# The third layer's recurrence by eights of chunks instead of chunk by chunk, with a new plan of the layer

## The chip, the cores and the metric

The kernel runs on one core of a Trainium2 chip. The metric is the device time of one execution in microseconds, as the median of several runs; a profiled execution gives the trace that is read here.

## The reference

One inference step of a network with four layers, on 128 context tokens and 512 latent tokens with 1,024 channels each (T = 640, E = 2,048). Every layer normalises its input, projects it, mixes the tokens in its own way, multiplies by SiLU(z), projects back and adds to the stream. The mixers are a Mamba-2 scan, a gated MLP over chunks, an S5 state-space layer, and neighbourhood attention. All is float32; each large product is done in three passes over split operands.

Only the third layer (S5) changes. For each of 128 groups of 16 channels there are 64 complex states, in two directions:

```python
bb = ...                         # the input matrix, discretised, per group and direction
drv = einsum('gnj,blgj->blgn', bb, seq)            # complex, in two real parts
drv[:, 0] += a * h0                                # the state from which the latent tokens start
s[l] = a * s[l - 1] + drv[l]                       # the recurrence over the tokens
y_d = einsum('gjn,blgn->blgj', c_re, s_re) - einsum('gjn,blgn->blgj', c_im, s_im)
y = gelu(y_forward + y_backward + d_skip * u)
y = y * sigmoid(y @ w_glu + b_glu) * silu(z)
```

The final states of the context are an output too.

## The kernel before

Tokens are taken in chunks of 8: 64 latent chunks and 16 of the context. TensorE takes each chunk's inputs to what they add to the states (`drive`), so that the recurrence runs over chunks only, with a to the power 8 (the tile `A8`). The 128 groups are worked in four quarters. A quarter's states lie in `S[(group of 2, state), direction, place, part, pair]`: on each partition 2 directions x 81 places x 2 parts x 16 pairs. `scan` is a generator of steps. A step of the latent chunks (`steps`, lines 1743 to 1753) is, for each direction, one product of the state (32 numbers) with both parts of A8 (64 results, tile `sl`, L1750) and two additions of 32 into the next place (L1753); all six are on VectorE, forward and backward in turn, and the next step needs them. There are 63 such steps in a quarter. Beside them GpSimd does the 16 steps of the context's chunks (`step`, tile `sc`: one product of 128, L1760, two additions of 64, L1762).

When a quarter's states are there, each of its four output matrices kt (8 groups) is made: `take` copies states into `zr` (ScalarE, one copy on GpSimd), `gen` makes the matrices from states to outputs by halves (`gx` and `gy`: seven operations of 512 elements on VectorE and five on GpSimd a kt, L1531 and L1544), `answer` multiplies on TensorE (L1805), `kernel` makes the response within a chunk (`KK`, eight DMAs to `tr`), and `within` multiplies (L1830), adds on VectorE (L1831) and applies GELU.

All this is laid beside the layer's large products (L314). A slot is one k tile of a product: six matmuls with 320 columns. `PLAN` gives the order of 28 of the first 32 products (16 of u, and z), 256 slots; the four last are z. The gate's products follow, 16 of them with 16 k tiles: the first 16 slots of these use y of matrices 0 to 7, the next those of 8 to 15. `put(slot, f)` puts a piece of work into the program after that slot. `SCAN5` has the first and last slot of each quarter's scan, `OUTS5` the slot o of a quarter's first output and the distance of the next ones, `OUT5` the slots of an output's parts after o, `IN5` those of a u product's loads (`ix`), transposes (`turn`) and drives after its end. TensorE, VectorE, ScalarE and GpSimd keep to the program's order in this layer; each runs until an operand is missing or a buffer isn't free. The numbers of buffers are `BG` (gx), `BM`, `BY` (gy) and `BI` (ix). The weights' parts (`whi` on ScalarE, `wlo` on GpSimd five times in six and on VectorE once) are made one product ahead. y goes to DRAM and comes back in another order (`load_y`, L1845, eight pairs of rows by 320-byte runs) for the gate.

Of the kernel before, what the change touches and what calls it, by code (L numbers as in the profile page):

```python
# [1 line left out]

# [29 lines left out]
# the steps of a layer's first product before the second's, by sides; a side's norm, by slots: the sums so far, the  # L32
# whole by tokens, by rows (the other side's from the next layer's beginning); its first operands; from where on the
# engines keep to the order
# [5 lines left out]
# token t of chunk c and place l in the third layer: column l * 80 + c, the latent chunks first  # L40
# [6 lines left out]
def reorder(perm, c, there, here):  # L47
    """A layer's columns of a part's tokens (0 the context's, 1 the latent ones), and these in the same order."""
    t0, t1 = ((0, TC), (TC, T))[c]
    if perm == 8:  # L50
        return there.rearrange("p (l c) -> p l c", l=8)[:, :, PERM[c]], here.rearrange("p (c l) -> p l c", l=8)
    there = there[:, t0:t1]
    if perm == -8 and c == 1:
        return there.rearrange("p (c r) -> p r c", r=8), here.rearrange("p (r c) -> p r c", r=8)
    return there, here
# [6 lines left out]
class Cut:  # L62
    """The tokens in two sides, between layers of these orders: the first side's last products come before the other's,
    and its next ones too. ys: a side's columns in the layer's order; hs: in the next's. A side's places are the natural
    order's: all has (first place, number, the columns of x, the places as these) for both parts; parts has them by part,
    with the next layer's columns; out: by part, with the products' columns in the layer's order."""

    def __init__(self, old, new):
# [19 lines left out]
        else:  # L88
            # the latent grid's columns from 32 on first
# [8 lines left out]
        if old == 8:  # L98
            # column l * 80 + r * 8 + q; in the natural order
# [18 lines left out]
class Net:  # L118
# [42 lines left out]
    def phase(self, name, side="left"):  # L161
        """A pool that lives as long as a part of a layer."""
# [5 lines left out]
    def x_tiles(self):  # L168
        """The residual stream, on the other side of the memory, from a layer's end into the next one."""
# [36 lines left out]
    def pcopy(self, o, a):  # L206
        """A copy on Pool."""
        self.nc.gpsimd.tensor_scalar(o, a, 1.0, 0.0, op0=OP.mult, op1=OP.add)

# [1 line left out]
    def raw(self, src, m=128):  # L211
        """src: a [128, 8, m] slice in DRAM."""
# [12 lines left out]
    def gemm(self, units, h, m=128):  # L225
        """units: weights' DRAM slices for the k tiles in eights; h(k) -> (hi, lo) [128, T]."""
# [15 lines left out]
    def stream(self, jobs, pairs=None, after=None, ahead=0, cut=None):  # L242
        """Products one after the other, the next weights' parts made ahead: jobs are (units, h, m, use), with
        use(the result). A generator, by k tiles. pairs: from there on, the first halves of two jobs come before their
        second ones. ahead: the weights' loads before their use. cut: the last product comes by sides, with use(the
        result, side)."""
# [76 lines left out]
    def play(self, jobs, at, pairs=None, also=(), after=None, cut=None, end=None):  # L323
        """The products, with other work (in program order) after some of their k tiles. also: other engines that
        keep to the program's order. after: the weights that are needed next."""
# [31 lines left out]
    def mod_w(self, i, nb, k, n, p, bufs, tag="wm"):  # L357
        """n k tiles' weights, from k on."""
# [4 lines left out]
    def mod_b(self, i, nb, q):  # L363
        """q [128, 4, 2]: a block's products."""
# [10 lines left out]
    def mod_pe(self, i, p, blocks=range(6), bufs=4, n=1):  # L375
        """On the tensor engine; a generator, by blocks."""
# [16 lines left out]
    def mod_ew(self, i, p, blocks=range(6), bufs=2, tags=("wm", "wacc"), pacc=None):  # L393
        """On the vector engine, but for turning the sums' partitions; a generator, in some more than four steps a
        block."""
# [43 lines left out]
    def put_beside(self, *work):  # L439
        """Work beside the present layer, by steps; the first layer's last modulation too, with its pool."""  # L440
# [4 lines left out]
    def tick(self, n):  # L445
        """Some steps of the work beside."""
        for g in self.beside:
            for _ in range(n):
                next(g, None)

# [1 line left out]
    def colsum(self, s):  # L452
        """s [128, T] -> the sums over its partitions, [token, chunk]."""
# [5 lines left out]
    def rowbc(self, r):  # L459
        """r [token, chunk] -> [128, T], the same on every partition."""  # L460
# [6 lines left out]
    def rstd(self, s, width):  # L467
        """s [128, T]: squares summed over the tiles -> 1/sqrt(mean + eps) on every partition."""
# [6 lines left out]
    def rstd_parts(self, s, width, out):  # L475
        """The same, into out; a generator, in two steps."""
# [7 lines left out]
    def rowcopy(self, r, out):  # L484
        """r [token, chunk] -> out [128, T], the same on every partition."""
# [11 lines left out]
    def square(self, k, t):  # L497
        """A tile's squares, to the sums over the tiles."""
# [18 lines left out]
    def enter(self, i, x, perm, ks):  # L517
        """The first layer's operands from its norm; the others' come with the layer before."""
# [19 lines left out]
    def side(self, i, x, s):  # L538
        """A side of the next layer's operands; a generator, by feature tiles."""
# [126 lines left out]
    def ordered(self, work):  # L666
        """In the program's order."""
# [5 lines left out]
    def norm_sums(self, s):  # L673
        """The squares' sums but for the last tile's."""
# [9 lines left out]
    def norm_tokens(self, s):  # L684
        """1/sqrt(mean + eps)"""
# [16 lines left out]
    def norm_rows(self, s):  # L702
        """The same on every partition."""
# [127 lines left out]
        # dt * decay to the end of the chunk (of the direction)  # L831
# [4 lines left out]
        # decay over a whole chunk, by step of the recurrence  # L836
# [6 lines left out]
        # decay by one token, to be broadcast: [dir, group, chunk, head, l]; none into a chunk's first token  # L843
# [1429 lines left out]
```

## Time and profile before

| | us |
|---|---|
| median of 3 runs | 3098.95 |
| lowest and highest | 3095.29, 3101.35 |
| profiled execution, first to last instruction (span) | 3088.6 |
| third layer, first u product to the gate's unbroken products | 1369 to 1953 |

The trace holds one execution; its time is given from the first instruction to the last. The runs' time is some 10 us longer, for what lies around these. Times in the rows below are microseconds from the span's start unless marked ns.

### The profile page before, as it was taken

What the parts mean: (1) busy time and instruction counts of PE and PEld (TensorE: products, weight loads), DVE (VectorE), ACT (ScalarE), POOL (GpSimd) and SP (SyncE); (2) the same over time, 40 slices, a digit from 0 to 9 for tenths busy, and PEclk for the clock granted to TensorE, in tenths of its full rate; (3) what the DMA queues carried; (4) which work ended last, traced back from release to release, by engine and by line L of the source; (5) the groups of instructions that cost most, each with busy time, mean ns of one, the idle gap of its engine ahead of it and who ended that gap; (6) DMA issues with size and microseconds to landing.
All of it is one profiled execution on the core that took longest, in us unless ns stands there. A gap on an engine that the chain in (4) does not pass through costs nothing.

```text
span 3088.6 us, 49942 instructions
## 1 busy us (share of the span) xinstructions
PE 2754.1 (89%) x18252; PEld 2663.7 (86%) x18252; DVE 2271.0 (74%) x5090; ACT 1319.5 (43%) x2359; POOL 1349.2 (44%) x1350
## 2 busy tenths in 40 slices
PE   7878887999989988989887867899999999999998
PEld 3868887889989988989887867899988999999988
DVE  7998777778789999983898893223965666667842
ACT  5422232331423333235545624445125666666641
POOL 4366656533276764443544543221434333333232
PEclk9989999999999999999988978899999999999999
DMA  6444334364433344545453536633634444444342
GB/s 249 121 128 118 115 107 116 99 219 161 150 112 126 124 143 154 194 148 184 133 178 116 161 109 149 148 108 102 201 121 128 134 133 135 135 135 135 109 174 86
DMA packets 248117, 432.17 MB, mean 140 GB/s; under 512 B 75264, under 2 KB 144320, under 8 KB 246848
## 3 DMA queue, kind: packets, MB, share of 16 engines
q1 hardware_dynamic: 247424, 427.66, 45.0%
q8 instruction: 145, 2.38, 0.3%
q0 software_dynamic: 448, 1.31, 0.1%
q14 instruction: 100, 0.82, 0.1%
HBM read 333.83 MB, written 65.70 MB: 129 GB/s over the span
## 4 chain that ended last, share of the span: by engine, by line
DVE 41%; PE 34%; issue 8%; ACT 8%; POOL 4%; DMA 4%; SPq 1%; DVEq 0%; ACTq 0%; POOLq 0%
PE acc L314 26%; DVE wacc L426 6%; DVE S L1753 4%; DVE cacc L902 3%; DVE sl L1750 3%; DVE wlo L204 2%; ACT whi L203 2%; DVE dd L1012 1%; DVE s5gx L1544 1%; DVE dd L1014 1%; DVE s5gx L1534 1%; POOL dd L1016 1%; ACT e L2054 1%; POOL dd L1009 1%; DVE Bu L1507 1%
## 5 line engine op out<-in xcount | busy, mean ns | idle before, releaser
L314 PE MATMUL acc<-hhi,whi 128*128 128x320 f32 (+2 forms) x3472 | 863.5, 328 | 27.9 <-DVE x L597 9.4
L314 PE MATMUL acc<-hhi,wlo 128*128 128x320 f32 (+2 forms) x3472 | 821.7, 316 | 10.8 <-DVE wlo L204 9.5
L314 PE MATMUL acc<-hlo,whi 128*128 128x320 f32 (+2 forms) x3472 | 824.0, 317 | 6.0 <-DVE hlo L566 3.7
L204 POOL TENSOR_TENSOR wlo<-raw,whi 128x1024 fp32r<-128x1024 f32 x157 | 400.2, 2551 | 694.9 <-ACT whi L203 681.0
L314 PEld LDWEIGHTS acc<-hhi,whi 128*128 128x128 f32 (+1 forms) x3472 | 602.4, 196 | 37.4 <-ACT hhi L203 16.6
L314 PEld LDWEIGHTS acc<-hhi,wlo 128*128 128x128 f32 (+1 forms) x3472 | 600.4, 193 | 14.5 <-DVE wlo L204 11.1
L314 PEld LDWEIGHTS acc<-hlo,whi 128*128 128x128 f32 (+1 forms) x3472 | 603.0, 194 | 10.4 <-DVE hlo L566 5.6
L203 ACT CAST whi<-raw 128x1024 fp32r<-128x1024 f32 (+1 forms) x289 | 300.4, 1046 | 423.4 <-PE acc L314 189.0
L426 DVE SCALAR_TENSOR_TENSOR wacc<-wm,conds,wacc 128x512 f32<-128x512 f32 x280 | 256.4, 971 | 0.3 <-DMA wm<-in_w_mod_dram 0.3
L314 PE MATMUL acc<-y,whi 128*128 128x320 f32 (+2 forms) x1024 | 202.5, 314 | 8.5 <-DVE y L204 4.5
L204 DVE TENSOR_TENSOR wlo<-raw,whi 128x1024 fp32r<-128x1024 f32 (+1 forms) x132 | 177.0, 1350 | 34.0 <-ACT whi L203 33.4
L1753 DVE TENSOR_TENSOR S<-S,sl 128x32 f32<-128x32 f32 x1008 | 189.9, 243 | 0.0
L314 PEld LDWEIGHTS acc<-y,whi 128*128 128x128 f32 x1024 | 163.6, 190 | 12.2 <-DVE y L204 5.7
L902 DVE SCALAR_TENSOR_TENSOR cacc<-pad,vec,cacc 128x644 f32<-128x644 f32 x128 | 138.1, 1079 | 1.1
L1009 POOL TENSOR_TENSOR dd<-cmat,dt 128x512 f32<-128x512 f32 x80 | 124.7, 1566 | 28.0 <-ACT dah L203 23.9
L1016 POOL TENSOR_TENSOR dd<-dd,dd 128x512 f32<-128x512 f32 x40 | 69.3, 1733 | 148.8 <-DVE dd L1014 148.8
L1534 POOL TENSOR_TENSOR s5gy<-Bu,Qt 128x512 f32<-128x512 f32 x64 | 90.3, 1431 | 90.3 <-DVE s5gx L1544 90.3
L1750 DVE TENSOR_TENSOR sl<-S,A 128x64 f32<-128x64 f32 x504 | 129.4, 297 | 0.0
L1868 DVE TENSOR_TENSOR y<-y,sg 128x640 f32<-128x640 f32 x16 | 14.1, 881 | 148.6 <-ACT sg L1867 148.6
L314 PE MATMUL acc<-y,wlo 128*128 128x320 f32 (+2 forms) x512 | 123.1, 312 | 0.0
L2087 DVE TENSOR_TENSOR yn<-yn,av 64x128 f32<-64x128 f32 x320 | 90.7, 284 | 43.0 <-ACT yn L2085 34.7
L2054 ACT ACTIVATE e<-sb,mx 128x384 f32<-128x384 f32 x128 | 78.9, 617 | 96.7 <-DVE mx L2053 94.8
(404 smaller groups left out, 5419.1 us busy)
## 6 DMA issues: line engine op xcount, KB each, us to landing
wm<-in_w_mod_dram SPq DMA_DIRECT2D x96, 512.0 KB, 3.9
raw<-in_w_out_dram SPq DMA_DIRECT2D x64, 512.0 KB, 4.3
raw<-in_w_nat_dram SPq DMA_DIRECT2D x64, 512.0 KB, 3.6
raw<-in_w_ssd_dram SPq DMA_DIRECT2D x48, 512.0 KB, 4.6
raw<-in_w_mlp_dram SPq DMA_DIRECT2D x48, 512.0 KB, 3.5
fb<-fd SPq DMA_DIRECT2D x40, 512.0 KB, 5.6
s5X<-s5gx SPq DMA_DIRECT2D x32, 512.0 KB, 2.6
raw<-in_w_s_dram SPq DMA_DIRECT2D x32, 512.0 KB, 4.4
```

What stands on the lines that cost most here:

```text
L203: (hi_eng or nc.scalar.copy)(hi, src)
L204: (lo_eng or nc.vector).tensor_tensor(lo, src, f(hi), op=OP.subtract)
L314: mm(p[:m, o:o + c], w[:, j, :], v(hx), start=(k == 0 and wi == 0), stop=(k == 8 * len(units) - 1 and wi == 2))
L426: e.scalar_tensor_tensor(acc[:, c], w[:, j], a, acc[:, c], op0=OP.mult, op1=OP.add)
L902: nc.vector.scalar_tensor_tensor(acc, pad[:, j:j + 644], w(j), acc, op0=OP.mult, op1=OP.add)
L1009: nc.gpsimd.tensor_tensor(dg.rearrange("p (h l) -> p h l", h=4), N.ident[:, None, :].to_broadcast([128, 4, 128]), self.dt[:, c, 32 * d + 4 ...
L1016: nc.gpsimd.tensor_tensor(ds[0], ds[0], ds[1], op=OP.add)
L1534: e.tensor_tensor(o.rearrange("p g (j l) -> p g j l", j=16), U[:, i, d, g, :, None].to_broadcast([128, 4, 16, 8]), Q[:, d, i, g, None, :]. ...
L1750: e.tensor_tensor(t[d], F[:, d, at[d], None, :].to_broadcast([128, 2, 32]), A[:, :, d], op=OP.mult)
L1753: e.tensor_tensor(dst[d], dst[d], t[d][:, k].rearrange("p (r g) -> p r g", r=2)[:, ::1 - 2 * k], op=OP.add)
L2054: nc.scalar.activation(e[:, :w], src, AF.Exp, bias=m[:, 1:2], accum_out=m[:, 2:3])
L2087: nc.vector.tensor_tensor(y[r, o], y[r, o], p[r, w:w + 128], op=OP.add)
```

## The change

A quarter's 64 latent chunks are taken as eight groups of eight, in both directions. `local(b)`, seven times, does a step within all eight groups at once: products of 8 x 64, additions of 8 x 32. `carry(a)`, six times, adds to the last place of a group what the last place of the group before gives, times the eighth power of A8. `spread(a, n, nb)`, seven times, adds to the places of a group what the last place of the group before gives, times the first seven (or, for the last group, eight) powers. The powers (`W8`, [128, 2, 8, 2, 32]) are made by GpSimd in each quarter, before the context's steps. The scan has 20 steps instead of 63, laid over 24 to 26 slots instead of 31 to 40. The plan of products, the places of scans and outputs, and the numbers of buffers change, and u is loaded for `within` after the output's beginning and no longer 15 slots ahead of it. Comments and docstrings are removed throughout; they are left out here.

```diff
-PLAN = "uuuuuzuuuzzzuuzuuzzuuuuzzzzz"
+PLAN = "uuuuuuuzuzzuuuuzuuuuzzzzzzzz"
-OUTS5 = ((80, 8), (139, 7), (188, 8), (228, 7))
-SCAN5 = ((43, 74), (96, 135), (148, 188), (196, 227))
+OUTS5 = ((72, 8), (114, 8), (164, 8), (214, 7))
+SCAN5 = ((44, 68), (84, 110), (134, 160), (184, 210))
 IN5 = (-3, -1, 1, 4, 9, 12)
-OUT5 = (-15, 0, -5, 0, 5, 7, 9, 17)
+OUT5 = (-15, 0, -2, 0, 5, 7, 9, 17)
-BG, BM, BY, BI = 3, 4, 2, 3
+BG, BM, BY, BI = 2, 4, 2, 2
...
-            for i in range(64):
-                put(a + (b - a) * i // 64, lambda N, g: next(g, None), scan)
+            for i in range(23):
+                put(a + (b - a) * i // 23, lambda N, g: next(g, None), scan)
...
                 put_(o + OUT5[0], self.load_out, P)
+                put_(o + 6, self.load_again, P)
...
+        W = self.tile(N, [128, 2, 8, 2, 32], "W8", 1)
...
+        def powers():
+            Wf = W.rearrange("p d b k (r g) -> p d b k r g", r=2)
             for k in range(2):
+                N.pcopy(Wf[:, :, 0, k, 0], A[:, k, :, 0:16])
+            yield
+            for b in range(1, 8):
+                t = self.tile(N, [128, 2, 2, 32], "sc", 1).rearrange("p d k (r g) -> p d k r g", r=2)
                 for d in range(2):
+                    g.tensor_tensor(t[:, d], Wf[:, d, b - 1, None, :, 0].to_broadcast([128, 2, 2, 16]),
+                                    A[:, :, d].rearrange("p k (r g) -> p k r g", r=2), op=OP.mult)
+                g.tensor_tensor(Wf[:, :, b, :, 0], t[:, :, 0], t[:, :, 1, ::-1], op=OP.add)
+                if b % 2:
+                    yield
+            Wf = W.rearrange("p d b k (r g) -> p (d b) k r g", r=2)
+            N.pcopy(Wf[:, :, 0, 1], Wf[:, :, 0, 0])
+            g.tensor_scalar(Wf[:, :, 1, 1], Wf[:, :, 1, 0], -1.0, 0.0, op0=OP.mult, op1=OP.add)
+            yield
...
-        for c in range(63):
-            steps(v, c, 63, None, "sl")
-            if c % 4 == 0:
-                i = 64 + c // 4
+        def context():
+            for i in range(64, 80):
                 step(g, i, 143, fin if i == 79 else None, "sc")
...
+                if i % 2:
+                    yield
+        def places(d, b, a0, n):
+            if d == 0:
+                return S[:, 0, 8 * a0 + b:8 * (a0 + n - 1) + b + 1:8]
+            return S[:, 1, 64 - 8 * (a0 + n - 1) - b:64 - 8 * a0 - b + 1:8]
+        def add(dst, t, dims):
+            for k in range(2):
+                for d in range(2):
...
+                    v.tensor_tensor(dst[d], dst[d], x, op=OP.add)
+        def local(b):
+            t = [self.tile(N, [128, 8, 2, 32], f"sx{d}", 1) for d in range(2)]
+            for d in range(2):
+                src = places(d, b, 0, 8).rearrange("p a r g -> p a (r g)")
+                v.tensor_tensor(t[d], src[:, :, None, :].to_broadcast([128, 8, 2, 32]), A[:, None, :, d].to_broadcast([128, 8, 2, 32]),
+                                op=OP.mult)
+            add([places(d, b + 1, 0, 8) for d in range(2)], t, 1)
+        def carry(a):
...
+                src = places(d, 7, a - 1, 1).rearrange("p a r g -> p a (r g)")
+                v.tensor_tensor(t[d], src[:, :, None, :].to_broadcast([128, 1, 2, 32]), W[:, None, d, 7], op=OP.mult)
+            add([places(d, 7, a, 1) for d in range(2)], t, 1)
+        def spread(a, n, nb):
...
+                v.tensor_tensor(t[d], src[:, :, None, :].to_broadcast([128, n, 2 * nb, 32]), w[:, None].to_broadcast([128, n, 2 * nb, 32]),
+                                op=OP.mult)
...
+            add(dst, [x.rearrange("p a (b k) x -> p a b k x", k=2) for x in t], 2)
+        todo = [lambda b=b: local(b) for b in range(7)]
+        todo += [lambda a=a: carry(a) for a in range(1, 7)]
+        todo += [lambda a=a: spread(a, 1, 7) for a in range(1, 7)] + [lambda: spread(7, 1, 8)]
+        beside = chain(powers(), context())
+        for f in todo:
+            next(beside, None)
+            f()
             yield
...
     def load_out(self, N, P):
-        P["ur"] = self.load_u(N, kt)
...
+    def load_again(self, N, P):
+        P["ur"] = self.load_u(N, P["kt"])
...
-        KK = self.tile(N, [128, 240], "KK", 2)
+        KK = self.tile(N, [128, 240], "KK", 1)
```

## Rows read from the trace of the kernel before

**Rows 1.** The page: the span, and the engines' busy time and share.
```profile
span 3088.6 us, 49942 instructions
...
PE 2754.1 (89%) x18252; PEld 2663.7 (86%) x18252; DVE 2271.0 (74%) x5090; ACT 1319.5 (43%) x2359; POOL 1349.2 (44%) x1350
```
**Rows 2.** Windows: length, busy (count) of PE, PEld, DVE, ACT, POOL; clock, DMA, GB/s.
```profile
1443.00:1509.00 66.00, 58.09 (x429) 57.60 (x428) 65.81 (x385) 28.13 (x54) 28.93 (x55) 0.96 0.46 142
1443.00:1886.00 443.00, 364.20 (x2546) 357.87 (x2546) 394.51 (x1675) 230.40 (x390) 230.08 (x309) 0.89 0.45 139
```
**Rows 3.** The chain of waits from 1443 to 1953, by line.
```profile
by line: DVE S L1753 27.1%; DVE sl L1750 17.7%; PE acc L314 8.4%; issue 6.7%; PE y L1805 6.0%; ACT zr L1601 5.8%; DMA gyl<-y5d 2.8%; DVE gx L1531 2.3%; SPq L1845 2.3%; PE t L1830 1.9%; DVE gx L1544 1.9%; PE drv L1717 1.9%; DMA hlo<-y5d 1.6%
```
**Rows 4.** Groups by line, 1443 to 1886: shapes, count | busy us, mean ns | idle before.
```profile
L1753 DVE TENSOR_TENSOR S<-S,sl 128x32 f32<-128x32 f32 x1008 | 189.9, 243 | 0.0
...
L1762 POOL TENSOR_TENSOR S<-S,sc 128x64 f32<-128x64 f32 x120 | 43.4, 362 | 9.4
```
**Rows 5.** Timeline of VectorE, GpSimd quiet: start, us, operation.
```profile
1470.91 0.35 DVE L1750 TENSOR_TENSOR sl<-S,A 128x64 f32<-128x64 f32 x2
...
1471.63 0.35 DVE L1750 TENSOR_TENSOR sl<-S,A 128x64 f32<-128x64 f32 x2
```
**Rows 6.** Timeline, VectorE and GpSimd: a weight's low part, then context steps.
```profile
1460.45 2.69 DVE L1753 TENSOR_TENSOR S<-S,sl 128x32 f32<-128x32 f32 x4
1460.71 2.39 POOL L204 TENSOR_TENSOR wlo<-raw,whi 128x1024 fp32r<-128x1024 f32 x1 [7.18 <-ACT whi L203]
...
1464.33 0.64 DVE L1750 TENSOR_TENSOR sl<-S,A 128x64 f32<-128x64 f32 x2
1464.43 0.45 POOL L1760 TENSOR_TENSOR sc<-S,A 128x128 f32<-128x128 f32 x1
...
1465.66 0.65 DVE L1750 TENSOR_TENSOR sl<-S,A 128x64 f32<-128x64 f32 x2
```
**Rows 7.** Timeline of VectorE: operations of 512 elements, GpSimd quiet.
```profile
1508.76 0.69 DVE L1531 TENSOR_TENSOR gx<-BC,PQ 128x512 f32<-128x512 f32 x1
1509.37 1.29 DVE L1544 TENSOR_TENSOR gx<-gx,gy 128x512 f32<-128x512 f32 x2
```
**Rows 8.** Timeline: VectorE's operations of 512 beside GpSimd's small and wide ones.
```profile
1548.05 0.95 DVE L1531 TENSOR_TENSOR gx<-BC,PQ 128x512 f32<-128x512 f32 x1
1548.53 1.38 POOL L1762 TENSOR_TENSOR S<-S,sc 128x64 f32<-128x64 f32 x2
1548.92 1.54 DVE L1544 TENSOR_TENSOR gx<-gx,gy 128x512 f32<-128x512 f32 x2
...
1861.02 1.54 DVE L1531 TENSOR_TENSOR gx<-BC,PQ 128x512 f32<-128x512 f32 x1
```
**Rows 9.** Last quarter: VectorE's wait for gx (timeline); two second answers (chain).
```profile
1854.88 3.13 DVE L1531 TENSOR_TENSOR gx<-BC,PQ 128x512 f32<-128x512 f32 x2 [1.47 <-PE y L1805]
...
1856.86 1.79 PE y L1805 x16
...
1868.46 1.77 PE y L1805 x16
```
**Rows 10.** The end: last output matrix, y's loads on SyncE (timeline); the gate (chain).
```profile
1884.03 2.13 DVE L1544 TENSOR_TENSOR gx<-gx,gy 128x512 f32<-128x512 f32 x2 [4.29 <-POOL gy L1531]
...
1928.82 17.97 SPq L1845 DMA_DIRECT2D gyl<-y5d  x32
...
1946.48 4.58 DMA gyl<-y5d
...
1952.77 7.31 PE acc L314 x48
```
**Rows 11.** A u product's transposes (timeline); ix loads from 1380 to 1445, to landing.
```profile
1390.34 1.03 PE L1692 MATMUL mT<-cmat,ix 128*128 128x128 f32 x8
...
1393.85 1.03 PE L1692 MATMUL mT<-cmat,ix 128*128 128x128 f32 x8
...
DMA to landing us min/median/max: 2.7/3.7/4.3
```

More of the change, by code (lines that the diff above doesn't have):

```diff
@@ L1 @@
 from contextlib import ExitStack, contextmanager
+from itertools import chain
 import numpy as np
@@ L1742, in scan @@
         yield
-        def steps(e, c, end, out, tag):
-            t = [self.tile(N, [128, 2, 32], f"{tag}{d}", 1) for d in range(2)]
-            at = c, end - c + 1
-            dst = [out[:, d] if out is not None else S[:, d, (c + 1, end - c)[d]] for d in range(2)]
-            for d in range(2):
-                e.tensor_tensor(t[d], F[:, d, at[d], None, :].to_broadcast([128, 2, 32]), A[:, :, d], op=OP.mult)
+        def powers():
+            Wf = W.rearrange("p d b k (r g) -> p d b k r g", r=2)
             for k in range(2):
+                N.pcopy(Wf[:, :, 0, k, 0], A[:, k, :, 0:16])
+            yield
+            for b in range(1, 8):
+                t = self.tile(N, [128, 2, 2, 32], "sc", 1).rearrange("p d k (r g) -> p d k r g", r=2)
                 for d in range(2):
-                    e.tensor_tensor(dst[d], dst[d], t[d][:, k].rearrange("p (r g) -> p r g", r=2)[:, ::1 - 2 * k], op=OP.add)
+                    g.tensor_tensor(t[:, d], Wf[:, d, b - 1, None, :, 0].to_broadcast([128, 2, 2, 16]),
[7 more added lines that the diff above has]
+            yield
         def step(e, c, end, out, tag):
@@ L1769, in scan @@
                     nc.sync.dma_start(N.O["s5"][:, q], fin.rearrange("p d r g -> p d (r g)"))
+                if i % 2:
[7 more added lines that the diff above has]
+                for d in range(2):
+                    x = t[d]
+                    x = (x[:, :, k] if dims == 1 else x[:, :, :, k])
+                    x = x.rearrange("p a (r g) -> p a r g" if dims == 1 else "p a b (r g) -> p a b r g", r=2)
+                    x = (x[:, :, ::1 - 2 * k] if dims == 1 else x[:, :, :, ::1 - 2 * k])
+                    v.tensor_tensor(dst[d], dst[d], x, op=OP.add)
@@ new lines, in local @@
+        def local(b):
[6 more added lines that the diff above has]
+        def carry(a):
+            t = [self.tile(N, [128, 8, 2, 32], f"sx{d}", 1)[:, 0:1] for d in range(2)]
+            for d in range(2):
+                src = places(d, 7, a - 1, 1).rearrange("p a r g -> p a (r g)")
+                v.tensor_tensor(t[d], src[:, :, None, :].to_broadcast([128, 1, 2, 32]), W[:, None, d, 7], op=OP.mult)
+            add([places(d, 7, a, 1) for d in range(2)], t, 1)
@@ new lines, in spread @@
+        def spread(a, n, nb):
+            t = [self.tile(N, [128, 8, 2, 32], f"sx{d}", 1).rearrange("p a b x -> p (a b x)")[:, 0:n * nb * 64]
+                 .rearrange("p (a b x) -> p a b x", a=n, x=32) for d in range(2)]
+            dst = []
+            for d in range(2):
+                src = places(d, 7, a - 1, n).rearrange("p a r g -> p a (r g)")
+                w = W[:, d, 0:nb].rearrange("p b k x -> p (b k) x")
+                v.tensor_tensor(t[d], src[:, :, None, :].to_broadcast([128, n, 2 * nb, 32]), w[:, None].to_broadcast([128, n, 2 * nb, 32]),
+                                op=OP.mult)
+                if d == 0:
+                    dst.append(S[:, 0, 8 * a:8 * (a + n)].rearrange("p (a b) r g -> p a b r g", b=8)[:, :, 0:nb])
+                else:
+                    x = S[:, 1, 65 - 8 * (a + n):65 - 8 * a].rearrange("p (a b) r g -> p a b r g", b=8)
+                    dst.append(x[:, :, ::-1][:, :, 0:nb])
+            add(dst, [x.rearrange("p a (b k) x -> p a b k x", k=2) for x in t], 2)
@@ L1770, in scan @@
+        todo = [lambda b=b: local(b) for b in range(7)]
[5 more added lines that the diff above has]
+            f()
             yield
+        for _ in beside:
+            pass
+        yield
     def load_out(self, N, P):
         nc, I, kt = N.nc, N.I, P["kt"]
-        P["ur"] = self.load_u(N, kt)
```

## The prediction

> **What bounds the kernel now.** I read the page first: TensorE is busy for 89% of the span and VectorE for 74%, and the number alone would call this a TensorE kernel [rows 1]. The change sits in the third layer, so the stage decides, not the average. In the windows by stage, from the first scan's start (1443) to the last output matrix (1886), VectorE is busy for 394.5 of 443 us and TensorE for 364; in the first scan alone VectorE has 65.8 of 66 us [rows 2]. The chain of waits agrees: from 1443 to 1953 the scan's two lines on VectorE, L1753 and L1750, hold 27.1% + 17.7% of the chain, some 228 us, and the products (L314) 8.4% [rows 3]. So in this stage TensorE waits for VectorE.
>
> The groups by line show that VectorE is not simply computing there. The scan's 1,008 additions of 32 elements average 243 ns [rows 4], but where GpSimd is quiet a whole step (two products, four additions) takes 0.72 us from one start to the next [rows 5]. Beside a context step on GpSimd (one product of 128 elements, two additions of 64) the step takes 1.33 us, and while GpSimd makes a weight's low part for 2.39 us, four additions take 2.69 us together [rows 6]. VectorE's operations do not wait in a gap here, they get longer: GpSimd's work is charged to VectorE's time. 63 steps at 0.72 are 45.4 us; the first scan's other 20 us are GpSimd's. I therefore treat VectorE's own time plus what GpSimd's instructions cost it as one budget.
>
> **The recurrence itself.** Before, a quarter has 63 x 0.72 = 45.4 us. After, it has seven local steps (two products of 512, four additions of 256), six carries (the shape of an old step), six spreads (two products of 448, four additions of 224) and one of 512 and 256. Two additions of 512 alone take 1.29 us together, the first some 0.69, so the other one adds 0.60 [rows 7]. A cost c + n s that gives 0.60 for n = 512 and 0.72 for an old step has c = 0.076 us and s = 1.023 ns: 0.338 for 256, 0.535 for 448, 0.306 for 224. Local steps: 7 x (1.20 + 1.35) = 17.9; carries 6 x 0.72 = 4.3; spreads 6 x (1.07 + 1.22) = 13.8; the last 2.55. Sum 38.5, so 6.9 us less a quarter, **-27.5** for four. Sixfold fewer steps save only 15%, since the elements have grown from 16,128 to 28,672, the spread being new work.
>
> **The context's 16 steps on GpSimd** stay, but now meet wide operations. With a GpSimd product of 128 elements beside it, a VectorE operation of 512 took 0.95 instead of 0.69, and two took 1.54 instead of 1.29 beside two GpSimd additions of 64 [rows 7, 8]. That is 0.27 + 2 x 0.125 = 0.52 a context step, against 1.33 - 0.72 = 0.61 before: 64 x 0.09, **-6** (0 if it stays at 0.61).
>
> **The powers W** are new on GpSimd: per quarter 21 operations of 64 elements, two copies of 32 and two of 256. At 0.125 for each small one, and 0.4 for each large copy (between 0.125 for 64 and 1.54 - 0.69 = 0.85 for 512 [rows 8]), they cost VectorE 2.6 + 0.25 + 0.8 = 3.7 us, **+15** for four. Below, 0: they run while VectorE is idle. Above, their own length: 23 x 0.36 [rows 4] + 2 x 0.85 = 10, so 40. I take the value that is nearest to measured neighbours of the same sizes. Their end is needed by the first carry; 25 operations alternate with the 42 of the local steps, so I see no wait there.
>
> The GPSIMD Engine Reference of the Trainium skill (section 1, Specifications) says that GpSimd's memory interfaces are shared with VectorE and contend with its instructions that have two SBUF inputs; rows 6 and 8 agree. Another page of the Trainium skill, Trainium Architecture — The Big Picture (section What this means for kernel authors) calls the shared pair an exclusive lock and not a split of bandwidth; by full lengths the powers would cost 40 and not 15 us. Rows 8 charge 0.125 of some 0.36 us.
>
> **Buffers.** gx goes from three buffers to two. Already now VectorE waits 1.47 us for TensorE's read of gx [rows 9]. With two, the matrices of an output's first half (slot o + 6) need the answer at o + 5, and the scan behind them in VectorE's order stands still. Where VectorE is behind TensorE, which is most of the stage, this costs nothing; I take **+5** for the four places where it follows a scan directly (0 to +35, below). ix goes from three to two: a half's first load can then go out only when the other half's first tile is transposed. The halves' transposes are 3.5 us apart, a load lands in 3.7 (2.7 to 4.3) [rows 11], so about 1 us a product; only the first quarter's four products and what precedes them delay the first scan, **+5** (0 to +8); later ones are under VectorE's budget, and would cost some 12 us if that were gone. KK with one buffer, and u loaded again later (11 slots of 0.9 us ahead of its use), I cost at nothing: the next response matrix comes a whole output later, 11.6 us [rows 9]. If that fails, the late thing is tr, and TensorE behind it.
>
> **The plan.** All 16 u products still come ahead of their scans, the number of products is unchanged, and the work on TensorE is only reordered: no gain of its own. The last quarter's outputs move from slots 228 to 249 to slots 214 to 235, so after the last output matrix TensorE has 14 more slots to do, while less of the outputs' traffic lies among the loads of y. Before, 66.6 us pass from that matrix (1884.03 + 2.13) to the first unbroken products at 1952.77 [rows 10]. After: seven slots (6.4 us at 7.31 for 48 products), an answer and a response (1.8 each) to slot 249; then SyncE issues the first four y loads and the last four, each four in the 18.0 us that the last took, the last lands 4.6 later, and some 1.6 pass to the next products (1946.48 + 4.58 to 1952.77): 10 + 42 = 52. That is -14 if nothing else is late and 0 if TensorE arrives behind; I take **-8**.
>
> **Sum.** -27.5 - 6 + 15 + 5 + 5 - 8 = -16.5. The profiled execution's span is 3088.6 us and the runs' median 3098.95; the 10 us outside the span do not change, so 3072 of span and **3082 us**.
>
> **Rivals.** (1) The gaps close too. VectorE is idle for 443 - 394.5 = 48.5 us between 1443 and 1886; shorter scans that start while the former quarter's outputs run (slot 84 instead of 96) could fill 25 of them instead of adding 5. Against: some idle time is spent in GpSimd's halves of the same matrices. It gives 3052.
>
> (2) Nothing is gained: each output is a chain of TensorE's answer, ScalarE's copies and the next answer, 11.6 us from one second answer to the next [rows 9]; if 4 x 4 of these and the products, and not the vector budget, set the new plan's pace, the net 18.5 us of the scan (27.5 + 6 - 15) become idle time: 3101. Against: VectorE at 89% of the stage.
>
> (3) Slower, by gx's two buffers. An output's matrices cost the budget 7 x 0.60 + 5 x 0.85 = 8.5 us; if each must wait for the chain of 11.6, some 2.5 us (a little goes to other work) stand idle 16 times, 40 us in place of the 5: 3117. It decides from 1.3 us an output on (21.5 / 16). For it: the 1.47 us above, with three buffers.
>
> (4) Slower, if wide VectorE operations make GpSimd's small ones cost their full length. Then the powers cost 40, and a context step 0.46 + 2 x 0.36 = 1.18 instead of 0.61 (64 x 0.57 = +36 instead of -6): 25 + 42 more, 3149. Rows 8 speak against it. This is the skill's exclusive lock taken at full length.
>
> **Numbers.** Forecast 0.43; rivals 0.20, 0.18, 0.12 and 0.07. A tenth of a per cent is noise here; I count 0.2%, 6.2 us, as the least that can be told from no change. The forecast's own range is 3068 to 3096: 0.39 of its 0.43 is faster. Rival 2 adds 0.02 faster and 0.14 same, rivals 3 and 4 with the last 0.02 are slower: faster 0.61, same 0.18, slower 0.21. The range leaves out rival 4, much of 3 and the end of 1: 3045 to 3112.
>
> **What would show it.** VectorE's new products of 512 near 0.68 us alone and the first scan near 60 us (it was 65); GpSimd's powers beside them and VectorE's operations 0.1 to 0.3 longer; VectorE still above 85% from the first scan to the last matrix; the first unbroken products of the gate near 1936 (1952.8 - 16.5). I am wrong if VectorE idles ahead of gx for TensorE's y (rival 3), if its products of 512 average well above 1 us in the local steps (rival 4), or if TensorE never waits in this stage (rival 1).

## The result and the profile after

| | before | after |
|---|---|---|
| median, us | 3097.12 | 3138.93 |
| lowest and highest, us | 3093.27, 3101.35 | 3136.86, 3141.78 |
| span of the profiled execution, us | 3088.6 | 3135.1 |

The ratio is 1.0135, with a 95% interval of 1.0123 to 1.0147: slower by 42 us. The forecast was 3082 with a range of 3045 to 3112, so both its sign and its range were wrong.

First the page of the changed kernel, which answers to [rows 1].

```profile
span 3135.1 us, 49026 instructions
...
PE 2767.8 (88%) x18252; PEld 2673.8 (85%) x18252; DVE 2221.6 (71%) x4058; ACT 1319.7 (42%) x2359; POOL 1439.5 (46%) x1450
```

VectorE has 49 us less to do than before and GpSimd 90 us more. The time was not lost by a busier VectorE. The windows (columns as in [rows 2]) say where: the first scan, then the stretch from its start to the last output matrix, then 38 us inside the fourth scan.

```profile
1451.00:1510.00 59.00, 50.32 (x351) 49.43 (x349) 58.65 (x127) 23.63 (x46) 43.87 (x77) 0.91 0.45 139
1451.00:1933.00 482.00, 360.41 (x2504) 351.75 (x2503) 345.36 (x643) 230.39 (x390) 315.41 (x406) 0.86 0.42 126
1820.00:1858.00 38.00, 6.71 (x29) 6.48 (x30) 20.15 (x51) 3.76 (x10) 24.66 (x56) 0.57 0.16 46
```

The first scan takes 59 us where it took 66, about as forecast. But the stage grew from 443 to 482 us while VectorE's busy time in it fell from 394.5 to 345.4: VectorE is now idle for 137 us of it, where it was idle for 48.5. In the third row nearly everything is quiet: TensorE is busy for 6.7 of 38 us, and its granted clock falls to 0.57, which is the lower of its two levels (1.2 GHz) for most of the time.

What they wait for stands in the waits of SyncE's queue (what the queue waited for: us in total, times, longest). The first row is the kernel before, the next ones the changed kernel from 1400 to 2003.

```profile
SPq L1769 <- POOL fin L1762: 7.1, 3, 3.4
```
```profile
SPq L1780 <- POOL fin L1774: 80.0, 4, 30.3
SPq L1849 <- DVE gx L1532: 69.5, 12, 14.5
SPq L215 <- POOL wlo L205: 59.4, 16, 14.3
```

L1780 is the store of the context's final states, `fin`, one small DMA a quarter. SyncE issues it itself, so it waits at it until GpSimd's last context step has run, and every DMA behind it in SyncE's queue waits too. The timeline of SyncE in the fourth quarter shows this, and then what TensorE was doing:

```profile
1817.96 0.33 SPq L1849 DMA_DIRECT2D BC<-in_s_c_dram  x1
1848.70 0.34 SPq L1780 DMA_DIRECT2D out_s_dram<-fin  x1
1849.09 0.42 SPq L1851 DMA_DIRECT2D PQ<-s5P  x1
1849.61 0.38 SPq L1853 DMA_DIRECT2D Br<-s5B  x1
1850.08 0.38 SPq L1675 DMA_DIRECT2D ur<-u5d  x1
1850.56 0.53 SPq L1910 DMA_DIRECT2D y5d<-r  x1
1851.18 5.07 SPq L1897 DMA_DIRECT2D tr<-KK  x8
...
1857.81 3.67 PE L1906 MATMUL t<-ur,tr 128*128 128x80 f32 x16 [28.21 <-DMA tr<-KK]
```

From 1818 to 1848.7 SyncE issues nothing. The eight DMAs from KK to tr, which have nothing to do with fin, follow the store; TensorE stands for 28.21 us at the response that needs tr, and in program order all of the large product is behind that response. VectorE's additions behind it wait as well (`r` for TensorE's `t`: 61.5 us in the stage, 14.9 before).

In the kernel before, SyncE issued eight DMAs from KK to tr ahead of the fourth quarter's store:

```profile
1832.53 5.27 SPq L1821 DMA_DIRECT2D tr<-KK  x8
...
1838.53 0.38 SPq L1769 DMA_DIRECT2D out_s_dram<-fin  x1
```

It is SyncE that comes earlier, and not GpSimd that is later. Counted from VectorE's copy to `fin` that opens a scan, SyncE came to the store 37, 71, 87 and 82 us later in the kernel before, and GpSimd was done at 41, 73, 88 and 81. In the changed kernel SyncE comes at 35, 34, 34 and 21 us, and GpSimd is done at 41, 60, 52 and 51.

### The profile page after: what moved, and what is told of

It is laid out like the page before. It is cut to its first block, busy times and chain, and to the rows that moved or that the text cites. A ratio compares the mean times of both kernels' runs of the same rounds, so it can differ in the third digit from the quotient of the medians.

```text
span 3135.1 us, 49026 instructions
## 1 busy us (share of the span) xinstructions
PE 2767.8 (88%) x18252; PEld 2673.8 (85%) x18252; DVE 2221.6 (71%) x4058; ACT 1319.7 (42%) x2359; POOL 1439.5 (46%) x1450
## 4 chain that ended last, share of the span: by engine, by line
PE 35%; DVE 35%; issue 10%; POOL 8%; ACT 7%; DMA 4%; SPq 1%; DVEq 0%; ACTq 0%; POOLq 0%
PE acc L315 27%; DVE wacc L427 6%; DVE cacc L903 3%; DVE wlo L205 2%; DVE S L1799 2%; ACT whi L204 2%; DVE dd L1013 1%; DVE dd L1015 1%; DVE s5gx L1545 1%; DVE s5gx L1535 1%; POOL dd L1017 1%; ACT e L2130 1%; POOL dd L1010 1%; DVE Bu L1508 1%; DMA wm<-in_w_mod_dram 1%
## 5 line engine op out<-in xcount | busy, mean ns | idle before, releaser
L205 POOL TENSOR_TENSOR wlo<-raw,whi 128x1024 fp32r<-128x1024 f32 x157 | 415.5, 2649 | 684.5 <-ACT whi L204 638.9
L1799 DVE TENSOR_TENSOR S<-S,sx 128x256 f32<-128x256 f32 (+2 forms) x320 | 133.4, 476 | 0.0
L1942 POOL TENSOR_TENSOR y<-y,z 128x640 f32<-128x640 f32 x16 | 25.2, 1574 | 173.1 <-ACT z L1940 173.1
```

Of the source, the lines that this page charges most:

```text
L205: (lo_eng or nc.vector).tensor_tensor(lo, src, f(hi), op=OP.subtract)
L1799: v.tensor_tensor(dst[d], dst[d], x, op=OP.add)
```

## The experiments

The theory: fin's store holds SyncE's queue, and that is the loss. Its rivals: the smaller buffers, GpSimd's powers, the plan, or a stage in which VectorE no longer sets the pace.

Times are medians. The kernel before was timed again beside each set of runs, on the same chip (medians of 3097.56, 3098.49, 3096.47, 3096.75 and 3094.99); the third column is the difference from that one, and all differences below are made of these. By the intervals each is good to some 3 to 5 us, those of e7, e9 and e17 to 6 to 8.

| kernel | us | against before, us | ratio, 95% interval |
|---|---|---|---|
| e1_store_late | 3145.91 | +48.4 | 1.0156, 1.0141 to 1.0171 |
| e2_store_pool | 3101.65 | +4.1 | 1.0012, 1.0003 to 1.0022 |
| e3_before_ctx | 3095.25 | -2.3 | 0.9989, 0.9976 to 1.0002 |
| e6_before_bufs2 | 3106.25 | +8.7 | 1.0024, 1.0013 to 1.0035 |
| e7_scans_earlier | 3118.54 | +20.1 | 1.0066, 1.0047 to 1.0086 |
| e8_new_scan_old_plan | 3097.13 | -1.4 | 1.0000, 0.9990 to 1.0011 |
| e9_old_scan_new_plan | 3121.82 | +23.3 | 1.0073, 1.0051 to 1.0095 |
| e10_before_store_pool | 3100.5 | +2.0 | 1.0005, 0.9993 to 1.0018 |
| e11_before_half_scan | 3027.65 | -68.8 | 0.9780, 0.9766 to 0.9795 |
| e12_no_spread | 3081.68 | -14.8 | 0.9958, 0.9944 to 0.9972 |
| e13_no_powers | 3093.66 | -2.8 | 0.9989, 0.9979 to 0.9998 |
| e14_old_plan_gx3 | 3098.27 | +1.8 | 1.0010, 0.9997 to 1.0022 |
| e15_last_outs_late | 3107.88 | +11.1 | 1.0042, 1.0030 to 1.0055 |
| e16_short_slots | 3099.98 | +3.2 | 1.0014, 1.0000 to 1.0027 |
| e17_short_slots_outs | 3119.73 | +23.0 | 1.0075, 1.0050 to 1.0101 |
| e18_gen_early | 3108.61 | +11.9 | 1.0037, 1.0024 to 1.0050 |
| e19_old_plan_wlo | 3095.68 | +0.7 | 1.0001, 0.9989 to 1.0012 |
| e20_store_pool_wlo | 3099.49 | +4.5 | 1.0011, 1.0000 to 1.0022 |

### The store of fin

**e1_store_late**: the call is moved to the end of the scan.

```diff
-                if i == 79:
-                    nc.sync.dma_start(N.O["s5"][:, q], fin...)
...
         for _ in beside:
             pass
+        nc.sync.dma_start(N.O["s5"][:, q], fin...)
         yield
```

> The changed kernel, but the store of the context's final states (fin) is put into the program after the scan's last step and no longer behind the context's last step. Theory A (SyncE's queue stands behind this store until GpSimd has done the context, 80 us in four waits, and the loads and tr transfers behind it come late): most of the loss comes back, 3075 to 3100, with the longest SyncE wait on fin below 5 us. Theory B (gx and ix in two buffers make VectorE and TensorE wait): no change, 3130 to 3142. Theory C (wide vector operations beside GpSimd's new work have used up the gain): no change, 3130 to 3142.

A miss, and one of the experiment: the trace has SyncE waiting for fin for 78.6 us (29.4 the longest), and the store stands at the same place among SyncE's DMAs in the first three quarters; in the fourth it comes two loads later, still ahead of the eight DMAs to tr. SyncE is not among the engines that keep to the program's order here, and where the call stands did not decide the place of its DMA. So this run says nothing against the store.

**e2_store_pool**: the store is issued by GpSimd, which makes fin.

```diff
-                    nc.sync.dma_start(N.O["s5"][:, q], fin...)
+                    nc.gpsimd.dma_start(N.O["s5"][:, q], fin...)
```

> The changed kernel, with the same store at its place but issued by GpSimd's own queue, where it stands behind the very work that it waits for. Theory A: as with the later store, 3075 to 3100, plus what GpSimd needs to issue four transfers (a few us). Theories B and C: 3130 to 3142.

37.7 of the 41.8 us come back with one word changed. SyncE no longer waits for fin at all. **e10_before_store_pool** makes the same edit in the kernel before:

> The kernel before with fin's store on GpSimd's queue and nothing else. Theory A (the store costs only where GpSimd is late): SyncE waited 7 us for fin, none of it on the chain, so within 4 us of 3097. If the store's queue were worth tens of microseconds by itself: 3060 to 3080.

There it changes nothing that can be measured, so GpSimd's queue is not better for the store in itself: the store was harmless where SyncE came to it 3.4 us early at most, and cost 38 us where it came 6.1, 25.5, 18.0 and 30.3 us early. **e3_before_ctx** put the context's steps into the first half of the old scan (`if c % 2 == 0 and c < 32: i = 64 + c // 2`), to move fin's end in the kernel before:

> The kernel before, with the context's 16 steps beside every second of the first 32 steps of a scan instead of every fourth of all 63, so that the store of fin comes earlier in SyncE's order while GpSimd's work is the same. Theory A: SyncE waits longer for fin (7 us in all before) and the kernel gets slower, 3100 to 3125, unless GpSimd is still done in time, which the wait on fin shows. Theories B and C: within 5 us of 3097.

SyncE's waits for fin stay at 3.4 us or less, so it made no test of the wait.

### The remaining terms, one at a time

**e6_before_bufs2** is the kernel before with the changed numbers of buffers.

```diff
-BG, BM, BY, BI = 3, 4, 2, 3
+BG, BM, BY, BI = 2, 4, 2, 2
...
-        KK = self.tile(N, [128, 240], "KK", 2)
+        KK = self.tile(N, [128, 240], "KK", 1)
```

> The kernel before with the changed numbers of buffers alone: gx 3 to 2, ix 3 to 2, KK 2 to 1. Theory B: it loses a large part of the 42 us, 3115 to 3140, with VectorE waiting for y ahead of gx (2.7 us before, 26.7 after). Theory A: up to 10 us slower, 3097 to 3107.

**e8_new_scan_old_plan** is e2 with PLAN, OUTS5, SCAN5 and OUT5 of the kernel before; **e9_old_scan_new_plan** is the kernel before with those of the change, its buffers, u's later load and the store on GpSimd.

> The changed kernel with fin's store on GpSimd's queue, and the plan of before (order of the products, places of scans and outputs); the buffers are the changed ones (two of gx and ix). Theory D: the new scan saves what it saves where the old plan keeps VectorE busy; the buffers cost 9: 3075 to 3095. Theory C: 3103 to 3120, the kernel before plus the buffers.

> The scan of before (63 steps, no powers) within the new plan: its order, places, buffers and the later load of u, with fin's store on GpSimd's queue. Theory D: the plan alone loses, 3115 to 3140, more than the new scan in it (3102), by the 13 to 25 us that the new scan saves. Theory C: 3097 to 3107, as the new scan in this plan.

The four together make a square, all with the smaller buffers, and with no block at the store. With the plan of before the new recurrence saves 10.1 us (8.7 to -1.4), with the new plan 19.2 (23.3 to 4.1). The new plan costs 14.6 us with the old recurrence and 5.5 with the new one. e8 lies between the two ranges expected of it. The square is not quite clean: e6 alone still loads u ahead of the output, and its store is still SyncE's (7.5 us of waits there). So the two steps out of e6 have u's later load in them. No run times that load alone; if it cost some 9 us, recurrence and plan would have one price each, 19.2 and 5.5. Each of the four differences is good to 4 to 8 us only.

### Is VectorE what the stage waits for?

**e11_before_half_scan** leaves out every second step of the latent chunks' recurrence in the kernel before; **e12_no_spread** leaves the spreads out of e2; **e13_no_powers** replaces the 21 small operations of the powers in e2 by a memset.

```diff
-            steps(v, c, 63, None, "sl")
+            if c % 2 == 0:
+                steps(v, c, 63, None, "sl")
```
```diff
-        todo += [lambda a=a: spread(a, 1, 7) for a in range(1, 7)] + [lambda: spread(7, 1, 8)]
+        todo += [lambda: None] * 7
```

> The kernel before, with every second step of the latent chunks' recurrence left out (31 of 63 in each quarter; the states of these chunks stay what the drives made them). That takes 31 x 0.72 = 22.3 us of VectorE's work out of a quarter, 89 us in all. If VectorE's time sets this stage, as the prediction took it, most of the 89 comes off: 3010 to 3040. If chains across the engines set the pace and VectorE is only busy while they run (rival 2), the saving turns to idle time: 3075 to 3095.

> The change with fin's store on GpSimd's queue (3101.65), and the seven spreads of each quarter left out (the states inside the groups lack what the group before gives). By the prediction's own price that is 13.8 + 2.55 = 16.4 us of VectorE's work a quarter, 65 us in all. By VectorE's budget: 3036 to 3060. By rival 2 (the outputs' chain and TensorE's order set the pace): 3085 to 3100.

> The change with fin's store on GpSimd's queue (3101.65), and the 21 small operations of the powers left out of each quarter on GpSimd; one memset of 448 elements writes a constant in their place, so the carries and spreads multiply by it. At the prediction's price (0.125 us of VectorE's time for each) 84 x 0.125 = 10.5 us come off: 3089 to 3093. At their full length (0.4 us each) 34 come off: 3068. If VectorE is not what the stage waits for: 3098 to 3103.

In the kernel before, 89 us of VectorE's work taken out at its undisturbed length gave 68.8 us: the premise was right there. In e2, 65 us taken out gave 18.9 us (4.1 to -14.8): not VectorE's budget, and a little more than rival 2 expected. (In the traces VectorE's busy time in the stage falls by 112 and by 79 us.) That the scan is shorter doesn't explain this by itself. In the stage from the first scan to the last output matrix e11 and e12 have nearly the same work on VectorE (282.7 and 272.9 us busy) and on TensorE (346.4 and 347.6), yet it takes 381 us in e11 (its window stands at the end of this text) and 422 in e12. What e12 has and e11 has not is the new plan, the smaller buffers, u's later load, and 69 us more work on GpSimd. The powers gave 6.9 us, where 84 times 0.125 is 10.5.

The windows of e2 and of e12 from the first scan to the last output matrix:

```profile
1455.00:1901.00 446.00, 352.82 (x2497) 345.29 (x2497) 352.04 (x643) 229.49 (x389) 315.09 (x409) 0.89 0.46 136
```
```profile
1454.50:1876.60 422.10, 347.55 (x2495) 341.39 (x2495) 272.90 (x475) 229.86 (x389) 302.56 (x409) 0.90 0.48 144
```

VectorE is idle for 94 us in e2 and for 149 in e12. The scans of e2 take 59, 77, 70 and 67 us, 62 us less than before in all (65.6, 86.3, 93.6, 90.0), and the gaps from a scan's end to the next one's start, or to the last output matrix, grew from 107 to 173 us. What fills a gap, the chain of waits of e2 between its second and third scan shows (start, us, what; "SPq" is SyncE's issuing):

```profile
1589.82 0.41 DVE r L1907
...
1591.39 3.20 PE acc L315 x12
1594.59 1.88 PE y L1881 x16
1596.47 1.78 PE acc L315 x12
1598.25 1.77 PE y L1881 x16
...
1600.91 1.75 PE drv L1719 x16
1602.66 0.89 PE mT L1694 x8
...
1603.56 3.41 DMA ix<-s5X
...
1608.06 1.55 SPq L1897
...
1614.44 0.53 SPq L1681
...
1615.07 3.58 DMA ix<-s5X
...
1618.79 0.63 PE mT L1694 x4
...
1622.03 1.80 PE acc L315 x12
1623.84 1.74 PE drv L1719 x16
```

VectorE is not in it from 1590.3 to the end of these lines. TensorE works the product, the former quarter's answers and the next quarter's transposes and drives in its order; then it waits for ix, whose loads SyncE issues behind the eight DMAs of L1897 (1608 to 1614). The next scan needs those drives.

### Can the plan be mended?

Eight runs try to find the plan's price or a version that beats both kernels. **e7_scans_earlier** (on e2: the last two scans from 132 to 154 and 172 to 196), **e15_last_outs_late** (on e2: only the last quarter's scan at 196 to 224 and its outputs from 228), **e18_gen_early** (on e2: `OUT5` with -5 again), **e16_short_slots** and **e17_short_slots_outs** (on e8):

```diff
-SCAN5 = ((43, 74), (96, 135), (148, 188), (196, 227))
+SCAN5 = ((43, 68), (96, 128), (148, 180), (196, 220))
...
-OUTS5 = ((80, 8), (139, 7), (188, 8), (228, 7))
+OUTS5 = ((74, 8), (132, 7), (182, 8), (222, 7))
```

(e16 has the first edit alone, e17 both.)

> The changed kernel with fin's store on GpSimd's queue, and two scans placed earlier: the third at slots 132 to 154 (was 134), the fourth at 172 to 196 (was 184); they can't come sooner for the drives that they need. Theory D (what is left of the loss once the store is out of SyncE's way is the plan: VectorE finishes a scan, then follows the outputs' chain for some 50 us before it begins the next scan): VectorE has the fourth scan beside the third quarter's outputs, 3080 to 3095. Theory C (the vector work itself isn't less): 3097 to 3107, as with the store alone (3102).

> The change with fin's store on GpSimd's queue (3101.65), and only the last quarter put where it was before: its scan from slot 196 to 224 and its outputs from slot 228 on, instead of 184 to 210 and 214 on. If the plan's price (4.5 to 15.5 us in the runs so far) lies in the last quarter's outputs, which come ahead of 14 slots of products: 3092 to 3097. If it lies in the places of the first three quarters: 3101 to 3110, since the last scan then starts later with nothing in return.

> The change with fin's store on GpSimd's queue (3101.65), and the first half of an output's matrices made five slots ahead of the output as before, instead of two. If the plan's price is that the answers wait for late matrices: 3092 to 3098. If two slots were enough, or two buffers of gx hold the earlier ones up anyway: 3100 to 3104.

> The new recurrence with fin's store on GpSimd's queue in the plan of before (3097.1), its scans laid over 25, 32, 32 and 24 slots instead of 31, 39, 40 and 31, from the same first slots; outputs where they were. If the old plan's long scans are what keeps the new recurrence from giving more than 9 us there: 3085 to 3093. If TensorE's own order between a scan's end and the next scan's start sets the pace: 3095 to 3099.

> As the kernel with the short scans in the plan of before, and the outputs follow six slots earlier (74, 132, 182 and 222 instead of 80, 139, 188 and 228). If the time of the outputs' chain after each scan is what counts, earlier outputs give some 6 slots of 0.9 to 1.5 us back where TensorE waits: 3082 to 3092, faster than both kernels. If moving outputs ahead only moves TensorE's waits, as in the plan of the change: 3096 to 3106.

None is faster, and e7, e17 and e18 came out above both ranges expected of them. Scans moved ahead cost 16 us over e2, the last quarter put back costs 7, and matrices made three slots earlier cost 8 (VectorE then waits 45.9 us for TensorE's read of gx instead of 25.7). On e8, scans over fewer slots cost 5, which is hardly clear of the intervals, and outputs six or seven slots earlier another 20.

**e14_old_plan_gx3** gives e8 three buffers of gx again (one tile for the products of both directions, and two buffers of u, make room). **e19_old_plan_wlo** and **e20_store_pool_wlo** let VectorE make a weight's low part twice in six (`WLO5 = "ppv"` instead of `"pppppv"`), on e8 and on e2.

> The new recurrence with fin's store on GpSimd's queue in the plan of before (3097.1), and three buffers for gx as before; the memory comes from one tile for the products of both directions (they are worked one after the other) and two buffers for u instead of three. If the 8 us that the smaller buffers cost the kernel before are gx's: 3087 to 3091, faster than both kernels. If they belong to ix or KK: 3095 to 3100.

> The new recurrence with fin's store on GpSimd's queue in the plan of before (3097.1), and VectorE makes a weight's low part twice in six instead of once. It takes some 14 of these (2.4 us each on GpSimd, 1.2 to 1.4 on VectorE) from GpSimd, which is busy 322.8 of 440 us here against 224.9 before, and gives them to VectorE, which has 86 us idle. If GpSimd's longer queue is the new limit: 3080 to 3090, faster than both kernels. If it is not: 3096 to 3104.

> The same in the plan of the change (the change with fin's store on GpSimd's queue, 3101.65). If GpSimd's queue is what takes the scan's saving there: 3085 to 3095. If the waits between TensorE, SyncE and VectorE do: 3099 to 3107.

Three null results (e14 3.2 us above e8, e19 2.1 above it, e20 0.4 above e2). The last two moved less than was expected of them: of the 29 low parts that GpSimd makes between 1369 and 1960, VectorE took over six and not 14. That is some 14 us of GpSimd's work, where e2 has 85 us more of it in the stage than the kernel before (315 and 230). So they don't rule GpSimd out as a limit. In e14 the directions are worked one after the other, and its scans take 68 to 92 us instead of e8's 56 to 85, so it doesn't price the third buffer cleanly.

## Why the prediction was wrong, by its own steps

**The step that failed: the part on the context's 16 steps on GpSimd.** It says that they "stay, but now meet wide operations", and charges them to VectorE alone. It counts the product and the two additions and leaves out the last thing that these steps issue, fin's store, and so the queue that stands behind it. The change had moved the store ahead against SyncE's other DMAs, while GpSimd was no later after a scan's start, and SyncE then stood for 80 us instead of 7. Shown by e2: 37.7 of 41.8 us. Nothing in the sum, its bounds or its rivals had this mechanism; that is why the range failed too. The trace of before had the row that would have put the question: SyncE already waits at L1769 for GpSimd.

**The plan, "no gain of its own … work on TensorE only reordered": wrong.** It costs 14.6 us with the old recurrence and u's later load in it, and 5.5 with the new one (e6 to e9, e8 to e2). Reordering is not free where four engines keep to one order: it moves the waits, and e7, e15, e17 and e18 each moved them for the worse. Which of its edits costs what is not settled.

**The recurrence: each cost right, its worth right in one plan and half of it in the other.** Where an operation follows another of its kind and GpSimd is quiet, 256 elements take 0.336 us in the trace of after (forecast 0.338), 448 take 0.536 (0.535), 224 take 0.302 (0.306). The first scan takes 58.4 us (forecast near 60). Beside GpSimd they are longer, as the groups by shape in the changed kernel show (busy us, mean ns):

```profile
L1799 DVE TENSOR_TENSOR S<-S,sx 128x256 f32<-128x256 f32 x128 | 69.8, 604 | 0.0
...
L1806 DVE TENSOR_TENSOR sx<-S,A 128x512 f32<-128x512 f32 x56 | 45.6, 852 | 0.0
L1799 DVE TENSOR_TENSOR S<-S,sx 128x224 f32<-128x224 f32 x96 | 41.3, 492 | 0.0
L1826 DVE TENSOR_TENSOR sx<-S,W 128x448 f32<-128x448 f32 x48 | 33.6, 740 | 0.0
```

The net of the three terms (-27.5, -6, +15) was -18.5. The runs give -19.2 in the new plan, and -10.1 in the old one with u's later load in it. No run prices the -6 alone. "Sixfold fewer steps" is a slip: 63 become 20, about a third; the sum doesn't use it. VectorE's time on the scan fell further, from 281.0 to 220.2 us, but not all of it reached the end.

**The powers, +15: near it, and far from their full length.** e13 gives 6.9 us for 84 of the 100 operations, 0.08 us each, against the 0.125 taken and the 0.5 to 0.6 us that one lasts on GpSimd in the changed kernel (56 of 599 ns on average, 28 of 472). VectorE's busy time on the page is 9.7 us less in e13 than in e2 (2218.8 and 2228.5), or 0.12 each; but the changed kernel, with the same operations as e2, has 2221.6, so neither price is sharp. The Trainium skill's Trainium Architecture — The Big Picture (What this means for kernel authors) calls the pair of ports that VectorE and GpSimd share an exclusive lock. If every one of these operations had held VectorE for its full length, that would have been 46.8 us (an estimate from the lengths above); e13 shows a seventh of it. Rival 4 falls: products of 512 average 0.85 us, not well above 1.

**Buffers, +10: right.** e6 measures 8.7 us for gx, ix and KK together. VectorE's wait for TensorE's read of gx rose from 2.7 to 26.3 us there and to 26.7 in the changed kernel, with far less lost at the end: rival 3's mechanism is there, at a fraction of its price. From the first u product's start to its 49th slot's the changed kernel takes 80.5 us, 77.3 before; that is the ix term (+5, 0 to +8), and e6, with the buffers alone, has 80.8. KK's one buffer and u's later load were put at nothing: TensorE waits 13.8 us for tr at the responses in e2 and 12.0 before, which shows no price, but no run takes them back alone.

**The tail, -8 (-14 to 0): within its bounds.** From the last output matrix to the gate's unbroken products it was 66.6 us [rows 10]. In the changed kernel it is 61.8 (1932.76 to 1994.54), in e2 62.8. These are its rows:

```profile
1931.48 1.28 DVE L1545 TENSOR_TENSOR gx<-gx,gy 128x512 f32<-128x512 f32 x2
...
1994.54 0.90 PE L315 MATMUL acc<-gyl,whi 128*128 128x320 f32 x2 [0.47 <-DVE gyl L205]
```

**The whole.** Step by step through the kernels that were run, the 41.8 us are +8.7 for the buffers, -10.1 for the recurrence with u's later load, +5.5 for the plan (with the tail in it) and +37.7 for the store. Along the other side of the square the recurrence has -19.2 and the plan, with u's later load, +14.6; what each is worth by itself these runs don't tell. Without the store's block the change is worth +4.1 us (1.0003 to 1.0022): no gain either. One statement of the sum was wrong without effect: the 10 us "outside the span". In every timed run here the time is 1.8 us above the span; so the profiled execution of before was a short one, by that 3090.4.

**Rival 2's number is what is left when the store is out of the way; its mechanism is so only in part.** It gave 3101 for the case that the vector saving turns to idle time; e2 has 3101.65. That the number fits so well is luck: rival 2 has the scan's saving worth nothing and +2 for buffers and tail, while the steps above have -10.1 for the recurrence against +14.2 for buffers and plan. The condition for the forecast, VectorE above 85% from the first scan to the last matrix, fails: 72% in the changed kernel, 79% in e2. But rival 2's chain, answer, copies, next answer, is only part of what the gaps show: e2's waits are spread over GpSimd's halves of gx (47.0 us of VectorE's time), TensorE's read of gx (25.7), the drives and the loads of ix. The text's own test "if TensorE never waits" was for rival 1, and TensorE waits.

**What stays open** is which of these the 62 us of shorter scans would have to be traded against. e12 shows that 65 us less of VectorE's work gives only 19, e19 and e20 that six weights' parts off GpSimd give nothing that can be measured, and no single wait that was tried holds it. GpSimd's work as a whole was not taken back in any run: e13 took 34 us of it (1441.6 to 1407.2 on the page) for 6.9. Why the store stands where it does among SyncE's DMAs wasn't tried beyond e1. No version with the whole computation beats the kernel before by more than the runs can tell; the new recurrence in the old plan (e8) equals it.

## What to carry to other kernels

A DMA that waits for a computing engine stops every DMA behind it on its queue: here SyncE issued nothing for 30.3 us while `fin` was not ready. When the engine's work is moved, its stores count as part of it: look in the trace at what the queue waits for now, and issue such a store from the engine that makes the data (here that gave 37.7 us). Moving the call in the program isn't enough where the queue is not held to the program's order; check the place in the trace.

A budget of the bounding engine holds for the kernel in which it was read. A change that takes work off that engine and alters the plan, the buffers and another engine's load with it can let other chains take over; a run with the work simply left out shows at once whether the budget still holds (69 of 89 us given back in the one kernel, 19 of 65 in the other).

## What the runs showed of the hardware

VectorE's cost of wide operations on float32 was linear to within 4 ns from 224 to 448 elements (0.302, 0.336 and 0.536 us, one behind the other with GpSimd quiet). What GpSimd adds to VectorE's operations did not grow with GpSimd's work: the old scan's 1,512 operations took 281.0 us where 181.6 was worked out for them alone (4 x 45.4), the new one's 480 took 220.2 where 154 was (4 x 38.5), so the addition fell from 99 to 66 us while GpSimd's busy time inside the four scans rose from 162 to 213 us. Whether that is the width of the operations or the shorter scans was not tested.

TensorE's granted clock followed its waits: 0.57 in the 38 us in which it was busy for 6.7, and 0.86 over the stage where it was 0.89 before [rows 2]. In e11, where TensorE is busy for 346 of 381 us, the same stage had 0.96:

```profile
1448.00:1829.00 381.00, 346.43 (x2552) 340.81 (x2551) 282.72 (x932) 232.01 (x390) 233.65 (x309) 0.96 0.54 162
```
